# Keys and queries stored in residue order for dilated attention, stores issued one step later, and the last tiles finished by feature quarters

## The chip, the core and the metric

The kernel runs on one core of a Trainium2 chip. The metric is device time in microseconds, the median of three runs. Engines are named as in the profile: PE is TensorE's matmul, PEld its weight load, DVE is VectorE, ACT is ScalarE, POOL is GpSimd, SP is the sync engine, whose queue issues nearly all DMAs of this kernel in order. L1077 is line 1077 of the kernel before the change. Beside the times there is one profiled execution, with its trace.

## What is computed

One layer of a hybrid decoder, in fp32, for a prompt of 2048 tokens and for eight single decode steps. The input projection gives attention queries, keys and values (6 heads of 64), the mLSTM's branch (4 heads of 160) and gates:

```python
z = rmsnorm(x, norm1_g) @ w_in
qa, ka, va, xb, ob, gates = jnp.split(z, SPLITS, axis=-1)
branches = [dilated_prompt(qa, ka, va, rel_bias, w, d) for (w, d) in ((128, 1), (512, 4), (2048, 16))]
out_a = rmsnorm(combine_branches(branches).reshape(B, S, D_A), attn_out_g)
```

A branch with dilation d regroups the positions by their residue modulo d. Within a residue, every block of 128 queries attends to its own block and the one before it, with a causal band, a relative-position bias and a softmax; the three branches are merged by their softmax denominators. The other half of the features goes through a causal convolution and an mLSTM in 16 chunks of 128 tokens. Both halves go through w_out, then a feed-forward part with squared ReLU (1024 to 4096 to 1024) and a last rmsnorm. Outputs are y for both inputs and the new caches (keys, values, convolution and mLSTM state).

## The kernel before

Matrix products in fp32 are made from fp32r parts: a value is split into a high and a low part (`split`), and `mm3` issues three matmuls, high by high, high by low and low by high. A tile framework allocates buffers by name with a number of slots, adds the semaphores and orders the instructions; instructions under `pinned` keep the program's order.

The work goes through these stages, in microseconds of the profiled execution:

- 0 to 103, `norm_and_v`: norm, transposes, values. Each of 16 tiles stores its values at once, to the scratch tensor `v_d` (65 columns a head, the last one 1.0) and to the output (L867, L868).
- 103 to 242, `project_qk` (L913 to L977): three 128-row weight tiles for keys, then three for queries, each over the six column blocks of `BLK` (344 or 340 tokens). A block is 24 matmuls into a PSUM slot (four slots). ACT copies it out, `split` or the like makes `hi` and `lo` (two buffers each), and two DMAs store them to `k_d` or `q_d`, which hold 384 rows by 2048 tokens in natural order, one tensor for the high and one for the low part. Keys are also transposed (`to_rows`, a block later) and stored as an output. The bias tables (`setup_bias`) and the gates (`setup_gates`) are made in between.
- 242 to 402, `xbob(0)`: the mLSTM's input and output-gate projections for the first 1024 tokens, with convolution and gates on DVE and ACT, and stores after each block (L1002, L1027, L1035, L1036); the decode steps' attention runs beside it.
- 402 to 578, `xbob(1)`: the same for the rest, with three steps of `attention` between its blocks.
- 578 to about 1025, `mlstm`: 16 chunks, with the rest of `attention` in between (0.72 attention steps a step of the mLSTM). A chunk loads its slices and two broadcast rows (`Mb`, `wr`), and stores its result `G2c` to `oB_d` (L491).
- 1009 to 1252: output projection, norm and transposes for the feed-forward part.
- 1252 to 2586: the feed-forward part by a seven-product scheme for 2 x 2 blocks (`PROD_A`, `PROD_B`, `PROD_C`), in two halves of tokens; pinned steps with a hand-written look-ahead (`ahead`), and background jobs (`bg`) popped between steps.
- 2586 to 2607: the last five tiles are finished.

`attention` goes over 6 heads, for each over branches 2, 1, 0 (dilations 16, 4, 1), for each over 4 groups of 4 tiles, two tiles a step. `load_head` loads a head's `Q2` (64 rows of the high part over 64 rows of the low part), `KH` (the high part twice) and `KL` (the low part twice), two buffers each, when the head before begins its last branch. `front` makes the scores of a tile with two matmuls of 256 columns (L1077) that pick the positions of a residue by a stride:

```python
mv, out, c0 = K[:, a - P * d:a + (P - 1) * d + 1:d], s_[:, e], 0
pe.matmul(out, Q[:, a:a + (P - 1) * d + 1:d], mv, start=i == 0, stop=i == 1)
```

Where a tile has only its own block (the first block of a residue, all tiles at dilation 16), two neighbouring residues are computed and one is used, to keep 256 columns. DVE adds the bias and takes the minimum (L1079), ACT takes the exponential (L1081), `turn` transposes on PE (L1090) and copies (L1092), `weigh` multiplies with `V` (L1105), and every fourth tile ACT copies to `R4` (L1107, three buffers) and a DMA stores it (L1108). A group's `V` is loaded at its start (L1128, four buffers). A step's weigh comes three steps after its scores.

At the end, the accumulator `acc` of the feed-forward part holds features by rows; a tile of 128 tokens is transposed back in two halves of 512 features and added to x (`half`, L1595 and L1597), then `final` takes the square sum (L1603), the root, the scaling by root and gain (L1609, or L1606 with L1607 on GpSimd for every second of the last five), and stores (L1610). The last product, number 7, completes features 0 to 511 of tiles 8 to 12; features 512 to 1023 of these tiles are complete after product 4 and are added in the background.

## Time and profile before

| | |
|---|---|
| median of three runs | 2617.8 us (2612.7, 2617.8, 2622.02) |
| profiled execution | 2609.03 us |
| its span, first to last instruction | 2607.3 us |
| mean granted TensorE clock | 0.982 |
| DMA traffic | 491.13 MB, mean 188 GB/s |

The profile lists for each engine its busy time; for a line and operation, the number of instructions, their busy time, their mean duration, and the idle time of the engine just before them with what ended it. A window gives busy time by engine in a stretch, the granted clock, the mean busy share of the 16 DMA engines and the rate. A busy matmul is counted from the start to a modelled end, so neighbouring ones overlap. The queue's own waits say what held SP back before it could issue.

### The profile page before, as it was taken

The page shows a single profiled execution, that of the slowest core. Times are in us where ns is not written, and L with a number is a line of the kernel's source. Part 1 is how long each engine was busy: PE and PEld are TensorE (multiplying, and loading weights), DVE is VectorE, ACT ScalarE, POOL GpSimd, SP SyncE. Part 2 cuts the span into 40 slices and gives each one's busy share as a digit, 9 for nine tenths or more (in the row PEclk, how much of TensorE's full clock was granted, in tenths as well). Part 3 has the DMA queues.
Part 4 walks back from the last instruction along what each step waited for, and adds up shares of the span by engine and source line. Part 5 has one row for each costly group of instructions (what it writes and reads, how often), then busy time and mean ns, then how long its engine had stood idle before and what let it go on. Part 6 is the DMA issues. An engine that isn't in the chain of part 4 may idle for free. (4 is left out here: it accounts for less than half of the span.)

```text
span 2607.3 us, 41900 instructions
## 1 busy us (share of the span) xinstructions
PE 2502.6 (96%) x15646; PEld 2259.5 (87%) x15646; DVE 1762.1 (68%) x3146; ACT 1190.7 (46%) x2324; POOL 861.9 (33%) x435
## 2 busy tenths in 40 slices
PE   8999999999999998999999999999999999999996
PEld 7989999997888886788788878877799999999995
DVE  6333755663876567664476997779868777776875
ACT  6331223433445544455566435553345643456333
POOL 1000000002432323211345775447743333543331
PEclk9999999998999998999999999999999999999998
DMA  7674656736768744865676868768576543765332
GB/s 200 156 194 150 178 137 175 186 98 150 186 174 190 170 127 140 269 221 169 211 263 213 289 226 273 234 207 296 205 265 240 186 133 96 241 216 170 109 118 74
DMA packets 471727, 491.13 MB, mean 188 GB/s; under 512 B 117399, under 2 KB 388147, under 8 KB 467812
## 3 DMA queue, kind: packets, MB, share of 16 engines
q1 hardware_dynamic: 469700, 484.84, 61.5%
q0 software_dynamic: 1536, 3.10, 0.5%
q8 instruction: 123, 2.02, 0.3%
q14 instruction: 80, 0.66, 0.1%
q10 hardware_dynamic: 288, 0.53, 0.1%
HBM read 379.97 MB, written 124.56 MB: 194 GB/s over the span
## 5 line engine op out<-in xcount | busy, mean ns | idle before, releaser
L74 DVE TENSOR_TENSOR al<-ax,ah 128x1024 fp32r<-128x1024 f32 x222 | 413.2, 1864 | 151.5 <-ACT ah L74 150.9
L74 POOL TENSOR_TENSOR ax<-ax,ay 128x1024 f32<-128x1024 f32 x117 | 313.6, 2682 | 309.1 <-DMA ay<-in_w_ff_dram 267.6
L1583 PE MATMUL pf<-bl,ah 128*128 128x258 f32 (+1 forms) x1344 | 361.1, 323 | 11.5 <-DVE bl L74 11.5
L1549 PE MATMUL pf<-bh,ah 128*128 128x258 f32 (+1 forms) x1344 | 360.4, 323 | 11.6 <-DVE R L74 11.1
L1549 PE MATMUL pf<-bh,al 128*128 128x258 f32 (+1 forms) x1344 | 357.9, 321 | 2.0 <-DVE al L74 2.0
L1583 PE MATMUL pf<-bh,al 128*128 128x258 f32 (+1 forms) x1344 | 358.9, 321 | 0.0
L1549 PE MATMUL pf<-bl,ah 128*128 128x258 f32 (+1 forms) x1344 | 358.3, 321 | 0.0
L1583 PE MATMUL pf<-bh,ah 128*128 128x258 f32 (+1 forms) x1344 | 351.9, 323 | 4.6 <-ACT bh L74 2.9
L74 ACT ACTIVATE ah<-ax 128x1024 fp32r<-128x1024 f32 x222 | 234.0, 1055 | 236.7 <-PE pf L1583 123.7
L74 POOL TENSOR_TENSOR bx<-R,R 128x1024 f32<-128x1024 f32 (+1 forms) x80 | 243.8, 3054 | 259.2 <-DVE bl L74 259.2
L74 DVE TENSOR_TENSOR bl<-bx,bh 128x1024 fp32r<-128x1024 f32 (+1 forms) x131 | 273.6, 2092 | 35.7 <-ACT bh L74 35.1
L1583 PEld LDWEIGHTS pf<-bl,ah 128*128 128x128 f32 x1344 | 225.4, 191 | 33.4 <-DVE bl L74 14.1
L1549 PEld LDWEIGHTS pf<-bh,ah 128*128 128x128 f32 x1344 | 224.6, 190 | 32.4 <-issue 10.2
L163 PE MATMUL pmm<-x,wh 128*128 128x344 f32 (+1 forms) x768 | 250.6, 326 | 0.0
L165 PE MATMUL pmm<-x,wl 128*128 128x344 f32 (+1 forms) x768 | 247.8, 323 | 0.0
L1583 PEld LDWEIGHTS pf<-bh,ah 128*128 128x128 f32 x1344 | 224.1, 190 | 27.1 <-ACT bh L74 3.8
L164 PE MATMUL pmm<-x,wh 128*128 128x344 f32 (+1 forms) x768 | 247.4, 322 | 0.0
L1549 PEld LDWEIGHTS pf<-bh,al 128*128 128x128 f32 x1344 | 224.2, 190 | 22.4 <-DVE al L74 2.7
L1549 PEld LDWEIGHTS pf<-bl,ah 128*128 128x128 f32 x1344 | 225.2, 191 | 19.4
L1583 PEld LDWEIGHTS pf<-bh,al 128*128 128x128 f32 x1344 | 224.7, 190 | 19.2
L74 ACT ACTIVATE R<-R 128x512 f32<-128x512 f32 (+1 forms) x256 | 161.1, 630 | 131.1 <-DVE R L74 127.1
L74 DVE TENSOR_TENSOR R<-R,pf 128x512 f32<-128x512 f32 (+1 forms) x256 | 164.9, 681 | 51.5 <-PE pf L1549 38.0
(472 smaller groups left out, 4845.0 us busy)
## 6 DMA issues: line engine op xcount, KB each, us to landing
ax<-in_w_ff_dram SPq DMA_DIRECT2D x184, 512.0 KB
ay<-in_w_ff_dram SPq DMA_DIRECT2D x120, 512.0 KB
sum_d<-ax SPq DMA_DIRECT2D x40, 512.0 KB
ax<-sum_d SPq DMA_DIRECT2D x40, 512.0 KB
xt<-in_x_prompt_dram SPq DMA_DIRECT2D x31, 512.0 KB
bx<-h_d SPq DMA_DIRECT2D x26, 516.0 KB
bx<-h_d SPq DMA_DIRECT2D x26, 512.0 KB
by<-h_d SPq DMA_DIRECT2D x22, 516.0 KB
```

The costliest lines, as they stand in the source:

```text
L74: return tc.keep_in_program_order(f(*a, **k))
L163: pe.matmul(out, lh, rh, start=first, stop=False)
L164: pe.matmul(out, lh, rl, start=False, stop=False)
L165: pe.matmul(out, ll, rh, start=False, stop=last)
L1549: pe.matmul(pf[:, n, :w], x_, y_[:, n * w:n * w + w], start=fst, stop=lst)
L1583: pe.matmul(pf[:, n, :w], x_[:, i, dsl], y_[:, n * w:n * w + w], start=a, stop=b)
```

## The change

- **Residue order.** `k_d` gets two versions, natural and regrouped by 16 residues within every 512 tokens; `q_d` gets three: natural, regrouped by 4 within 512, and regrouped by 16 over all 2048. `project_qk` makes them with copies on ACT (high part) and DVE (low part) and stores them all. The column blocks become 512 wide (the last one 256 and 264, with the eight decode tokens).
- **Attention reads.** The weights of a score matmul are always `Q[:, a:a + P]`, contiguous. Keys of dilation 4 and 16 are read in runs of 32 elements. At dilation 4 the keys then come in another order within a block, so `V` is loaded by four DMAs in that order, and the bias is reordered by one ACT copy a head.
- **Loads.** Q is loaded once a branch, K twice a head, each at group 1 of the branch before. `V` is loaded a group ahead (six buffers).
- **Stores later.** A class `Stores` holds store DMAs and issues them one step later in the projections (`vst`, `qst`, `xst`), in attention (`rst`) and in the mLSTM (`obs`). `R4` gets four buffers, `G2c` three, `wr` two; the transposed keys `kt` get one.
- **The end.** For tiles 8 to 12 the square sum is taken by parts (`sq3`). Features 512 to 1023 are added after product 4, features 0 to 255 after the first half of product 7's steps, with GpSimd multiplying both by the gain; features 256 to 511 are left for the end. One root serves all five tiles; the scaling is one instruction a tile, three on DVE and two on ACT. Up to three background jobs a step instead of two.

```diff
-    q_d = [dram.tile([DA, S], F32, name=f"q{x}_d") for x in "hl"]
-    k_d = [dram.tile([DA, S], F32, name=f"k{x}_d") for x in "hl"]
+    q_d, k_d = ([[dram.tile([DA, S], F32, name=f"{y}{x}{v}_d") for x in "hl"] for v in range(n)]
+                for y, n in (("q", 3), ("k", 2)))
+    class Stores:
+        def put(self, dst, src):
+            self.held.append((dst, src))
+        def go(self):
+            for dst, src in self.held:
+                nc.sync.dma_start(dst, src)
+            self.held = []
...
-        G2 = wk.tile([P, 5, P], F32, name="G2c")
+        G2 = wk.tile([P, 5, P], F32, name="G2c", bufs=3)
-            wr = wk.tile([P, H, P], F32, name="wr", bufs=1)
+            wr = wk.tile([P, H, P], F32, name="wr")
-        nc.sync.dma_start(cm_(oB_d)[:, :, ts], G2)
+        obs.put(cm_(oB_d)[:, :, ts], G2)
...
+                    for c0, n in ((0, 512),) if g < 3 else ((0, 256), (256, 264)):
+                        ps = proj(psm, "mm", wh, wl, b0 + c0, n)
+                        if not c0:
+                            qst.go()
+                        if later:
+                            to_rows(*later.pop())
...
+                    d = 16 if which == "k" else 4
+                    hd_ = ev.tile([P, 512], F32R, name="qhd")
+                    ld_ = ev.tile([P, 512], F32R, name="qld")
+                    act.activation(on(hd_, d), by(hi, d).bitcast(F32), AF.Copy)
+                    vec.tensor_copy(on(ld_, d), by(lo, d).bitcast(F32))
+                    for v, two in enumerate(((hi, lo), (hd_, ld_))):
+                        for dd, tt in zip(dst[v], two):
+                            qst.put(dd[j * P:(j + 1) * P, b0:b0 + 512], tt.bitcast(F32))
+                    if which == "q":
+                        if g == 3:
+                            q16 = [ev16.tile([P, 16, P], F32R, name=f"q16{x}") for x in "hl"]
+                        act.activation(q16[0][:, :, 32 * g:32 * g + 32], by(hi, 16).bitcast(F32), AF.Copy)
+                        vec.tensor_copy(q16[1][:, :, 32 * g:32 * g + 32], by(lo, 16).bitcast(F32))
...
-                    if w == 256:
-                        mv, out, c0 = K[:, a - P * d:a + (P - 1) * d + 1:d], s_[:, e], 0
+                    q = Q[:, a:a + P]
+                    if b == 0:
+                        mv = K[:, max(a - P, 0):max(a - P, 0) + 256]
+                    elif b == 1:
+                        g, t = a // 512, a % 512 // P
+                        if w == 256:
+                            mv = g44(K)[:, g - 1:g + 1, :, t]
+                            out = out.rearrange("p (k r z) -> p k r z", k=2, r=4)
...
+                        mv = g4(K)[:, :, a // P - e:a // P - e + 2].rearrange("p g r z -> p r g z")
-                    pe.matmul(out, Q[:, a:a + (P - 1) * d + 1:d], mv, start=i == 0, stop=i == 1)
+                    pe.matmul(out, q, mv, start=i == 0, stop=i == 1)
...
+                    if g == 1:
+                        if b:
+                            qq = load_q(h, b - 1)
+                        if b == 2:
+                            kk[0] = load_k(h, 0)
+                        elif b == 0 and h + 1 < HA:
+                            nb, kk[1], qq = load_bias_of(h + 1), load_k(h + 1, 1), load_q(h + 1, 2)
+                    V, vnext = vnext, load_group(*groups.pop(0)) if groups else None
+                    R4 = wk.tile([P, 4, HD + 2], F32, name="R4", bufs=4)
...
+            if ready and p == 7 and d["ds"][0] == 2 and not d["end"]:
+                bg.extend(ready)
+                ready.clear()
-            for _ in range(2 if sb and c and ph == 2 else 1):
+            for _ in range(3 if sb and c and ph == 2 else 1):
...
+                    def most(t, add=add):
+                        add(t, (0, 1))
+                        for xv, gv in ((xts[t][:, :256], fg[:, :256]), (xts[t][:, 512:], fg[:, 512:])):
+                            gp.tensor_tensor(xv, xv, gv, op=OP.mult)
...
                     for t in early:
-                        half(xts[t], acc, base, t, 0)
-                        final(xts[t], t, t % 2 == 1)
+                        add(t, (2, 3))
+                    v = small.tile([P, NE], F32, name="rs_v5")
+                    vec.tensor_tensor(v, sq3[:, 0], sq3[:, 1], op=OP.add)
+                    vec.tensor_tensor(v, v, sq3[:, 2], op=OP.add)
+                    vec.tensor_scalar(v, v, 1.0 / D, EPS, op0=OP.mult, op1=OP.add)
+                    r = rsqrt(v, P, NE)
+                    for t in early:
+                        xv = xts[t][:, 256:512]
+                        vec.tensor_tensor(xv, xv, fg[:, 256:512], op=OP.mult)
+                    for t in early:
+                        x_, k = xts[t], t - 8
+                        if k % 2:
+                            act.activation(x_, x_, AF.Copy, scale=r[:, k:k + 1])
+                        else:
+                            vec.tensor_scalar(x_, x_, r[:, k:k + 1], None, op0=OP.mult)
+                        nc.sync.dma_start(O["y_prompt"][0, t * P:t * P + P], x_)
```

More of the change, by code (lines that the diff above doesn't have):

```diff
@@ new lines, in project_qk @@
+                for g in (range(4) if which == "k" else (3, 0, 1, 2)):
+                    b0 = 512 * g
+                    hi = ev.tile([P, 512], F32R, name="qhi")
+                    lo = ev.tile([P, 512], F32R, name="qlo")
+                    qb = None
+                    if which == "k" or g == 3:
+                        qb = ev.tile([P, 520], F32, name="qb", bufs=3)
+                    for c0, n in ((0, 512),) if g < 3 else ((0, 256), (256, 264)):
[4 more added lines that the diff above has]
+                            to_rows(*later.pop())
+                        m = min(n, 512 - c0)
+                        cs = slice(c0, c0 + m)
+                        if which == "k":
+                            act.activation(qb[:, c0:c0 + n], ps[:, :n], AF.Copy)
+                            split(hi[:, cs], lo[:, cs], qb[:, cs])
+                        else:
+                            act.activation(hi[:, cs], ps[:, :m], AF.Copy, scale=-0.125)
+                            vec.scalar_tensor_tensor(lo[:, cs], ps[:, :m], -0.125, hi[:, cs].bitcast(F32),
+                                                     op0=OP.mult, op1=OP.subtract)
+                            if n > m:
+                                act.activation(qb[:, 512:], ps[:, m:n], AF.Copy, scale=-0.125)
+                    d = 16 if which == "k" else 4
[7 more added lines that the diff above has]
+                    if which == "q":
+                        if g == 3:
+                            q16 = [ev16.tile([P, 16, P], F32R, name=f"q16{x}") for x in "hl"]
+                        act.activation(q16[0][:, :, 32 * g:32 * g + 32], by(hi, 16).bitcast(F32), AF.Copy)
+                        vec.tensor_copy(q16[1][:, :, 32 * g:32 * g + 32], by(lo, 16).bitcast(F32))
+                        if g == 2:
+                            for dd, tt in zip(dst[2], q16):
+                                qst.put(dd[j * P:(j + 1) * P], tt.rearrange("p r z -> p (r z)").bitcast(F32))
+                    if qb is not None:
+                        later.append((which, j, g, qb))
@@ L1001, in xbob @@
                 vec.tensor_copy(halo[:, j], xb[:, m:m + 3])
-                nc.sync.dma_start(xbT_d[j * P:(j + 1) * P, b0:b0 + m], xb[:, 3:3 + m])
+                xst.put(xbT_d[j * P:(j + 1) * P, b0:b0 + m], xb[:, 3:3 + m])
                 c = ev.tile([P, 344], F32, name="c")
@@ L1060, in rows, with load_v @@
             return bass.AP(tensor=t.tensor, offset=t.offset + row * rs + off, ap=[[st[0], P], [st[1], 4], [1, w]])
+        def load_v(V, b, g, h):
+            if b == 1:
+                rs = HD + 1
+                for r in range(4):
+                    nc.sync.dma_start(V[32 * r:32 * r + 32],
+                                      bass.AP(tensor=v_d.tensor, offset=v_d.offset + (h * S + 512 * g + 4 * r) * rs,
+                                              ap=[[16 * rs, 32], [rs, 4], [1, rs]]))
+            else:
+                nc.sync.dma_start(V, rows(v_d, b, g, HD + 1, h * S * (HD + 1), HD + 1))
         def front(hd, b, tiles):
-            nb, Q, KH, KL = hd
-            d = BRANCHES[b][1]
+            nb, (KH, KL), Q = hd
             o, bw = NBW[b]
+            g4 = lambda t: t.rearrange("p (g r z) -> p g r z", r=16, z=32)
+            g44 = lambda t: t.rearrange("p (g k r z) -> p g k r z", k=4, r=4, z=32)
             ex = wk.tile([P, 2, 256], F32, name="ex", bufs=3)
@@ L1107, in weigh, with load_group @@
                 act.activation(R4[:, :, :HD + 1], po, AF.Copy)
-                nc.sync.dma_start(dst, R4)
-        hd = load_head(0)
+                rst.put(dst, R4)
+        nb, kk, qq = load_bias_of(0), {1: load_k(0, 1)}, load_q(0, 2)
         pend, turned, acc_o, DEPTH = [], [], [None], 2
+        rst = Stores()
+        def load_group(h, b, g):
+            V = wk.tile([P, 4, HD + 1], F32, name="V", bufs=6)
+            load_v(V, b, g, h)
+            return V
+        groups = [(h, b, g) for h in range(HA) for b in (2, 1, 0) for g in range(4)]
+        vnext = load_group(*groups.pop(0))
         def flush():
@@ L1149, in attention @@
             flush()
+        rst.go()
         yield
@@ L1193, in mlstm @@
                 next(cur)
+                if not i:
+                    obs.go()
                 if i and prev is not None:
@@ L1642, in phase_c @@
         copies = cache_copies()
-        bg = []
+        NE = 5
+        sq3 = pc.tile([P, 3, NE], F32, name="sq3")
+        bg, ready = [], []
         acc = None
```

166 lines of the change are left out of this document (81 added, 85 removed).

## The prediction

> **What bounds the kernel now.** I read the page first, then busy time by stage, then the score matmuls of attention by themselves, then the sync queue's own waits, and last the end of the span. The page gives the span
>
> ```profile
> span 2607.3 us, 41900 instructions
> ```
>
> and the busy time, share and instructions of each engine:
>
> ```profile
> PE 2502.6 (96%) x15646; PEld 2259.5 (87%) x15646; DVE 1762.1 (68%) x3146; ACT 1190.7 (46%) x2324; POOL 861.9 (33%) x435
> ```
>
> TensorE is busy for all but 105 us. That says only that it rarely sits idle: a matmul that reads its operands slowly is busy too. So the question for each stage is whether TensorE leaves time over there, and whether its work gets shorter. Stages, with the sync and DMA side in the last two columns (share of the 16 DMA engines, GB/s):
>
> ```profile
> core 0: us, PE busy (x) PEld busy (x) DVE busy (x) ACT busy (x) POOL busy (x), PEclk, DMA share, GB/s
> 103.00:242.00 139.00, 133.45 (x856) 130.36 (x856) 37.23 (x108) 39.12 (x103) 4.68 (x9) 0.99 0.62 172
> 242.00:402.00 160.00, 159.25 (x1031) 158.44 (x1031) 102.59 (x247) 40.63 (x76) 0.00 (x0) 0.98 0.60 170
> 402.00:580.00 178.00, 176.48 (x1146) 172.49 (x1145) 107.62 (x381) 66.58 (x150) 3.06 (x6) 1.00 0.57 144
> 580.00:700.00 120.00, 111.39 (x708) 92.13 (x707) 67.24 (x241) 51.81 (x154) 34.30 (x33) 0.90 0.66 159
> 700.00:850.00 150.00, 144.74 (x1010) 130.65 (x1010) 105.65 (x359) 75.93 (x238) 55.20 (x49) 0.99 0.76 188
> 850.00:1000.00 150.00, 141.55 (x1004) 127.57 (x1002) 89.03 (x313) 72.38 (x218) 39.16 (x36) 0.98 0.57 140
> ...
> 2400.00:2586.00 186.00, 178.98 (x1460) 177.37 (x1459) 136.18 (x138) 65.63 (x78) 56.94 (x18) 0.98 0.30 97
> 2586.00:2607.00 21.00, 3.32 (x23) 2.19 (x21) 12.30 (x29) 8.74 (x22) 5.25 (x2) 0.70 0.31 125
> ```
>
> 103 to 242 projects keys and queries, 242 to 402 is the first half of the other projections, 402 to 1000 holds attention (beside the second half of the projections, then beside the mLSTM), 2586 to 2607 is the tail after the last FFN matmul. Added over its four rows, attention keeps TensorE busy 574 of 598 us and VectorE 370: TensorE is the bound, and a microsecond taken from its work there is nearly a microsecond of the span.
>
> **Part 1: scores read in residue order.** Attention's score matmuls (L1077) are the same in number and shape in all three branches; only the strides differ. Their busy time, summed over six stretches, one a head, with dilation 16:
>
> ```profile
> sum 200.40, PE 71.06 PEld 49.68; mean PE 11.84 PEld 8.28
> ```
>
> with dilation 4:
>
> ```profile
> sum 193.80, PE 73.94 PEld 51.56; mean PE 12.32 PEld 8.59
> ```
>
> and with dilation 1:
>
> ```profile
> sum 199.80, PE 49.46 PEld 31.17; mean PE 8.24 PEld 5.19
> ```
>
> One head at dilation 4 (min/median/max ns, first and last start):
>
> ```profile
> L1077 PE MATMUL ps_s<-KL,Q x16: 407/416/422, 424.8 to 457.8; 128*128 128x256 f32 x16
> L1077 PEld LDWEIGHTS ps_s<-KL,Q x15: 332/332/335, 426.4 to 457.6; 128*128 128x128 f32 x15
> ```
>
> and at dilation 1:
>
> ```profile
> L1077 PE MATMUL ps_s<-KL,Q x17: 278/282/418, 457.8 to 490.8; 128*128 128x256 f32 x17
> L1077 PEld LDWEIGHTS ps_s<-KL,Q x16: 187/192/193, 458.4 to 490.7; 128*128 128x128 f32 x16
> ```
>
> A strided matmul takes 416 instead of 282 ns, its weight load 332 instead of 192. After the change the queries of every branch are contiguous, and the keys of dilations 4 and 16 come in runs of 32. If both branches then cost what dilation 1 costs, the saving is 71.06 + 73.94 - 2 x 49.46 = 46.1 us. No row shows runs of 32, so the bounds are the two rows above: 282 ns (all 46.1 saved) and 416 ns (nothing saved). I take the near end: 31 of 32 steps are the unit steps of the 282 ns row, and the extra 134 ns over 256 columns, 0.5 ns a strided step, would add 4 ns for eight jumps.
>
> The Trainium skill, page "SBUF — State Buffer", section "Door 1: The DMA port swizzle", states 16-byte lines and that four fp32 can be strided for free. Read so, stride 4 would have nothing to give and the saving would be 71.06 - 49.46 = 21.6 us; the 416 ns row at stride 4 contradicts it, and the measurement decides.
>
> What comes late next is VectorE's bias-and-minimum (L1079), which frees the score buffers. Idle time before L1077 from 402 to 1000, matmul and weight load added up:
>
> ```profile
>   DVE R L1079: 21.3, 27
> ```
>
> Nearly all of it lies in the dilation-1 stretches, where scores are already quick; counted twice by that row, it is some 10 us for the engine. Dilation 4 has the same tiles of 256 keys and will show the like, dilation 16 half the keys and little: I give back 6 us (0 to 10). Net of part 1: -40.
>
> **Part 2: the projection of keys and queries.** For each of six weight tiles, six blocks of up to 344 columns become three of 512, one of 256 and one of 264: 24 matmuls of 144 fewer, but the same columns. A 344-column matmul takes 160 / 1031 = 155 ns (row 242 to 402), 0.45 ns a column; a 512-column one in the FFN
>
> ```profile
> 1252.00:1410.00 158.00, 157.93 (x689) 127.35 (x688) 108.55 (x110) 100.33 (x156) 72.11 (x28) 1.00 0.72 238
> ```
>
> 229 ns, 0.45 ns too. Time goes by columns, so I count 1 us saved (0 to 22, if it went by number). VectorE and ScalarE get the reordering copies. Nearest rows:
>
> ```profile
> L160 DVE TENSOR_TENSOR qlo<-qb,qhi 128x344 fp32r<-128x344 f32 (+1 forms) x18 | 9.4, 522 | 44.5 <-ACT qhi L159 27.1 <-DMA kl_d<-qlo 17.3
> L956 ACT ACTIVATE qb<-pmm 128x344 f32<-128x344 f32 (+1 forms) x18 | 8.2, 456 | 41.6 <-PE pmm L165 41.6
> ```
>
> Per 512 columns that is about 0.75 us; 36 copies on each engine (12 key blocks, 24 for queries) make 27 us, on VectorE 37 + 27 of 139, on ScalarE 39 + 27. Even at twice the price TensorE covers them: nothing on the path.
>
> The stores are another matter. Keys go out twice and queries three times, each as high and low part of 384 x 2048 fp32 (3.15 MB): 31.5 MB instead of 12.6. The stage moves 172 GB/s at a share of 0.62, so its full rate is 277 GB/s, and 18.9 MB more are 68 us of all engines against 0.38 x 139 = 53 us free. The stage is then DMA-bound by up to 15 us, unless stores drain into the next one, whose share is 0.60. The row of L160 above already shows 17.3 us of VectorE waiting for a store to land without TensorE stopping (four PSUM slots lie between). I take +7 (0 to 23, the upper end with 8 us for weights of the next stage that queue behind the last stores).
>
> **Part 3: loads of attention.** Before, a head loads KH and, with the same counts, KL, and Q from its high and its low part:
>
> ```profile
> KH<-kh_d SPq DMA_DIRECT2D x12, 512.0 KB
> ...
> Q<-qh_d SPq DMA_DIRECT2D x6, 512.0 KB
> ```
>
> That is 6 x 0.524 = 3.15 MB a head. After: three Q and two pairs of K, 14 transfers, 7.34 MB; 25.2 MB more over six heads. Two wider windows:
>
> ```profile
> 402.00:1000.00 598.00, 574.16 (x3862) 522.85 (x3860) 369.54 (x1292) 266.70 (x758) 131.72 (x123) 0.97 0.64 157
> 712.00:867.00 155.00, 149.93 (x1031) 135.08 (x1031) 105.34 (x365) 75.67 (x236) 52.77 (x48) 0.99 0.76 182
> ```
>
> 157 GB/s at 0.64 is 245 GB/s at full share: 103 us more, on 0.36 x 598 = 215 us free. On average the share goes to about 0.87. From 712 to 867 it is 0.76 already, and 1.7 heads' worth of loads there would fill it. I charge +8 (0 to 25) for loads that come late in that stretch.
>
> **Part 4: stores one step later, V a group ahead, second buffers.** The sync queue issues in order, and a store that waits for its data holds the loads behind it. Its own waits from 580 to 1000:
>
> ```profile
> SPq L1108 <- ACT R L1107: 62.1, 18, 7.4
> SPq L491 <- POOL G2c L490: 50.7, 13, 6.9
> SPq L1128 <- PE po L1105: 38.6, 14, 6.1
> SPq L405 <- POOL wz L434: 21.0, 7, 7.0
> ```
>
> Those are the attention and mLSTM stores, the V load (four buffers, now six) and the decay row (one buffer, now two): all four are what the change moves. The queue gets some 48 more K and Q transfers and 72 more V transfers (dilation 4 in four pieces), which it has time for once 172 us of waiting shrink. TensorE sat idle 8.6 + 5.3 + 8.5 = 22 us in those stages (120 - 111.39, 150 - 144.74, 150 - 141.55), not all of it from late loads; I take -4 (0 to -12). From 242 to 580 TensorE idles 2.3 us, so the delayed projection stores win nothing there. Nothing computes longer because a store goes later: the store's tile is held one step longer, and G2c and R4 get a buffer more for it.
>
> **Part 5: the end in feature quarters.** Tail of before:
>
> ```profile
> L1603 ACT ACTIVATE jkc<-R 128x1024 bf16<-128x1024 f32 x5 | 5.3, 1050 | 19.9 <-DVE R L1597 19.9
> L1607 POOL TENSOR_TENSOR R<-R,g 128x1024 f32<-128x1024 f32 x2 | 5.3, 2626 | 31.9 <-ACT R L1606 31.9
> L1609 DVE SCALAR_TENSOR_TENSOR R<-R,rs_o,g 128x1024 f32<-128x1024 f32 x3 | 3.9, 1285 | 0.1
> L1597 DVE TENSOR_TENSOR R<-R,ptp 128x512 f32<-128x512 f32 x5 | 3.3, 684 | 0.7 <-PE ptp L1595 0.6
> L139 DVE TENSOR_SCALAR rs_v<-ss 128x1 f32<-128x1 f32 x5 | 0.8, 150 | 0.6 <-ACT jkc L1603 0.6
> ```
>
> and its last instruction by time:
>
> ```profile
> 2600.05 2.38 POOL L1607 TENSOR_TENSOR R<-R,g 128x1024 f32<-128x1024 f32 x1 [1.66 <-ACT R L1606]
> ```
>
> The last multiply ends at 2602.4, 4.9 us before the span does (the store). New tail after the last matmul at about 2586.3: the last put into the accumulator and transposes 1.2; five adds of 256 features at about 0.4, 2.0; the last square of a quarter row 0.65; one root for all tiles, nine small steps at 0.15 to 0.2, 1.8; five gain multiplies of 256 at 0.35, 1.8; scaling, three tiles on VectorE at no more than 1.29, 3.9, with two on ScalarE beside them; the store 4.9. Together 16.3 instead of 21.0. GpSimd multiplies three quarters of each tile, 0.75 x 2.63 = 2.0 us, 10 for five, hidden behind the last two steps (48 matmuls each at 178.98 / 1460 = 0.12 us, 5.9 us) and the adds; without that cover 4 us of it would show. Ten transposes move ahead of the last matmul (1.4 us at the 3.32 / 23 of the row 2586 to 2607), but three background jobs a step instead of two end the earlier tiles sooner, where TensorE now idles 7 us (186 - 178.98). I take -5 (+1 to -10).
>
> **Sum.** -46 + 6 - 1 + 7 + 8 - 4 - 5 = -35 us. The profiled execution took 2609.0 us, 1.7 of it outside its span, so it would become 2574. The runs shown have a median of 2617.8, 8.8 above it; the prediction for the median is 2617.8 - 35 = 2583.
>
> **The rivals.** *The transfers stay hidden and waits vanish.* For it: shares on average below 0.9, and a sync queue that no longer blocks. Against: 712 to 867. -46 - 1 - 8 (tail) - 7 (idle) = -62: 2556.
>
> *Slower: loads queue behind bursts.* Per head there are two bursts of 3.15 MB (keys of the next order with queries), 12.9 us each at 245 GB/s. Whatever is issued behind one, V or an mLSTM chunk's tiles, lands that much later; the lead is one group, a quarter of a dilation's 193.80 / 6 = 32 us, 8 us. If the consumers really have no more lead than that, each of 12 bursts stops TensorE for 5 us: +60, and with +15 in the projection the sum is -46 + 6 - 1 + 15 + 60 - 4 - 5 = +25: 2643. It decides where a burst is longer than the lead. For it, GpSimd waits for mLSTM loads today:
>
> ```profile
> POOL Mb L399 <- DMA Mb<-MtT_d: 64.7, 11, 32.9
> ```
>
> Against: V is used some three half groups after its scores, so its lead is nearer 20 us, and today's burst at a head's start is as long.
> The Trainium skill, "SBUF — State Buffer", same section, gives a 64-partition transfer only half of the ports, 196 GB/s at 1 MiB; each K and Q transfer has 64 partitions, and a burst would be an estimated 16 us. No view here isolates such a transfer.
>
> *The runs of 32 cost what strides cost.* Then part 1 is 0 and the rest +5: 2623.
>
> **How the numbers follow.** This measurement tells about 0.3% from no change, 7.9 us: below 2610 is faster, above 2626 slower. Forecast (-22 to -50 us, 2568 to 2596): 0.60. All hidden: 0.13. A smaller gain (2596 to 2610), where DMA takes half: 0.08. Bursts decide: 0.11, from +8 up in nearly all of it. Runs as slow as strides: 0.08, mostly within 0.3%. Faster 0.81, same 0.08, slower 0.11. The range, 2556 to 2612, leaves out the last two cases and a little of the second.
>
> **What would show it.** Right: score matmuls of all branches near 282 ns and about 150 us in three sums of 49; the stretch from 402 to 1000 some 40 us shorter with VectorE busier in share; DMA share near 0.9 there and above 0.85 from 103 to 242; the span's end some 16 us after the last FFN matmul. Wrong: score matmuls still above 350 ns (runs), or TensorE idle growing by over 30 us between 402 and 1000 with GpSimd or VectorE waiting for loads (bursts), or the projection of keys and queries over 155 us.

## The result, and the profile after

The change makes the kernel slower: 2641.3 us, median of 4 runs (2636.0 to 2644.5), against 2617.7; ratio 1.0108, 95% interval 1.0086 to 1.0129. The prediction said 2583 and faster. The profiled execution took 2644.5 us. Page of the kernel after, span and busy time:

```profile
span 2642.8 us, 41794 instructions
PE 2495.9 (94%) x15496; PEld 2216.9 (84%) x15496; DVE 1741.1 (66%) x3173; ACT 1236.8 (47%) x2345; POOL 875.4 (33%) x443
```

TensorE is 6.7 us less busy than before, in a span that is 35.5 us longer: the work shrank and the idle time grew. The stretch from the first to the last score matmul (402 to 995 before, 416 to 1044 now), first before, and then after, there with the two stages ahead of it and the end:

```profile
402.00:995.00 593.00, 569.16 (x3827) 517.96 (x3825) 366.62 (x1284) 265.80 (x756) 131.72 (x123) 0.97 0.64 158
```

```profile
103.00:256.00 153.00, 149.07 (x798) 125.69 (x797) 57.30 (x139) 74.28 (x108) 4.69 (x9) 0.97 0.80 259
256.00:416.00 160.00, 153.96 (x963) 151.95 (x962) 101.42 (x242) 43.40 (x77) 0.00 (x0) 0.95 0.70 192
416.00:1044.00 628.00, 555.24 (x3799) 489.30 (x3798) 352.67 (x1279) 270.17 (x759) 129.13 (x121) 0.90 0.78 187
2626.00:2643.00 17.00, 2.36 (x14) 1.15 (x12) 8.05 (x23) 6.17 (x18) 1.41 (x2) 0.69 0.39 154
```

The first score comes 14 us later (402.5, then 416.7), the score stretch takes 35 us more, and what follows the last score takes 13 us less (1612.1, then 1598.7), of which 4 are the end (no run shows where the other 9 come from). In the score stretch TensorE's idle time goes from 23.8 to 72.8 us, its granted clock from 0.97 to 0.90, and the share of the DMA engines from 0.64 to 0.78. Yet the score matmuls themselves did what they should. Their busy time over the whole stretch (TensorE, then weight load), before and after:

```profile
402.00:995.00 593.00, 194.05 (x576) 132.29 (x576) 0.97 0.64 158
```

```profile
416.00:1044.00 628.00, 143.84 (x576) 94.42 (x576) 0.90 0.78 187
```

That is 50 us less, even at a lower clock, and the median score matmul with the low part of the keys takes the 282 ns of dilation 1 (min/median/max over all branches):

```profile
L1146 PE MATMUL ps_s<-KL,Q x288: 277/282/582, 416.9 to 1043.9; 128*128 128x256 f32 x144
```

So the forecast gain is there, and something took it and 35 us more. One gap shows how. The sync queue of the kernel after, with the start and length of each issue (rows between left out), and TensorE:

```profile
500.73 0.45 SPq L1097 DMA_DIRECT2D Q<-qh_d  x1
506.87 0.37 SPq L146 DMA_DIRECT2D R_d<-R  x1
507.29 0.50 SPq L1098 DMA_DIRECT2D Q<-ql_d  x1
...
510.07 0.45 SPq L1098 DMA_DIRECT2D KL<-kl_d  x1
510.58 0.68 SPq L1120 DMA_DIRECT2D V<-v_d  x1
```

```profile
516.00 0.33 PE L1159 MATMUL pt<-ident,ex 128*128 128x128 f32 x1
523.65 1.94 PE L1175 MATMUL po<-V,pT 128*128 128x65 f32 x8 [7.33 <-DMA V<-v_d]
```

Inside the burst of queries and keys the queue stands 5.7 us until a store can go (from 501.18 to 506.87), then issues the rest, and V behind it (issued at 510.58) lands 13 us later, at 523.5. TensorE stands 7.33 us, and starts again at half clock with the DMA engines full:

```profile
510.00:516.00 6.00, 5.93 (x48) 5.39 (x46) 3.66 (x19) 3.79 (x12) 0.00 (x0) 1.00 0.97 220
516.00:523.60 7.60, 0.33 (x2) 0.13 (x1) 0.43 (x1) 0.22 (x1) 0.00 (x0) 0.73 1.06 220
523.60:530.00 6.40, 4.60 (x16) 4.01 (x17) 2.36 (x2) 2.36 (x3) 0.00 (x0) 0.50 1.06 271
```

Only few gaps are as plain as this one. The waits of the score stretch, kernel after (total, times, longest):

```profile
POOL hb L493 <- DVE hrd L490: 96.6, 12, 22.1
POOL Mb L413 <- DMA Mb<-MtT_d: 59.8, 9, 14.2
PE ps_s L1146 <- DVE R L1148: 32.0, 34, 3.8
PE po L1175 <- DMA V<-v_d: 10.8, 3, 7.3
```

TensorE's own longest wait is for VectorE's bias-and-minimum (L1148): 32.0 us here, 8.8 before. VectorE is busy 352.67 us of 628, so it waits in its turn, and the view doesn't say what stands first in that row. GpSimd's wait for the mLSTM's loads (`Mb`) hasn't grown: it is 59.8 us here, and the prediction shows 64.7 before.

### The profile page after: what moved, and what is told of

It is laid out like the page before. It is cut to its first block, busy times and chain, and to the rows that moved or that the text cites. A ratio compares the mean times of both kernels' runs of the same rounds, so it can differ in the third digit from the quotient of the medians.

```text
span 2642.8 us, 41794 instructions
## 1 busy us (share of the span) xinstructions
PE 2495.9 (94%) x15496; PEld 2216.9 (84%) x15496; DVE 1741.1 (66%) x3173; ACT 1236.8 (47%) x2345; POOL 875.4 (33%) x443
## 5 line engine op out<-in xcount | busy, mean ns | idle before, releaser
L74 DVE TENSOR_TENSOR al<-ax,ah 128x1024 fp32r<-128x1024 f32 x222 | 396.3, 1788 | 169.4 <-ACT ah L74 168.6
L175 PE MATMUL pmm<-x,wh 128*128 128x344 f32 (+4 forms) x720 | 245.6, 341 | 2.4 <-ACT wh L171 2.4
L177 PE MATMUL pmm<-x,wl 128*128 128x344 f32 (+4 forms) x720 | 243.4, 338 | 0.6 <-DVE wl L172 0.6
L176 PE MATMUL pmm<-x,wh 128*128 128x344 f32 (+4 forms) x720 | 242.4, 337 | 0.0
L1150 ACT ACTIVATE ex<-sm,R 128x256 f32<-128x256 f32 (+1 forms) x288 | 128.1, 458 | 170.9 <-DVE R L1148 146.6
```

The lines of the kernel that those rows point to most:

```text
L74: return tc.keep_in_program_order(f(*a, **k))
L175: pe.matmul(out, lh, rh, start=first, stop=False)
L176: pe.matmul(out, lh, rl, start=False, stop=False)
L177: pe.matmul(out, ll, rh, start=False, stop=last)
L1150: act.activation(ex[:, e, :w], sm[:, :w], AF.Exp, bias=mn, scale=-1.0)
```

## The experiments

Three theories. **Transfers**: the 25.2 MB of extra key and query loads make other transfers late, TensorE stands, and its clock falls in the gaps. **Chains**: shorter scores only uncover the mLSTM's root and VectorE's queue; the loads don't matter. **Held buffers**: a store one step later holds its buffer and reorders the queue. All runs; the stretch is from the first to the last score matmul, with TensorE's busy time, clock and the DMA share in it. A ratio compares with runs of before made beside that kernel; their median was 2617.7 beside after and 2607.6 to 2613.5 beside the others. So where the text takes the difference of two medians of different rounds, it can be off by some us:

| kernel | median us | ratio to before, 95% | stretch | busy | clock | DMA |
|---|---|---|---|---|---|---|
| before | | | 402 to 995 | 569 | 0.97 | 0.64 |
| after | 2641.3 | 1.0108 (1.0086, 1.0129) | 416 to 1044 | 555 | 0.90 | 0.78 |
| loads once | 2584.5 | 0.9893 (0.9870, 0.9917) | 415 to 975 | 523 | 0.95 | 0.68 |
| reads only | 2570.8 | 0.9842 (0.9817, 0.9867) | 401 to 956 | 524 | 0.96 | 0.67 |
| end only | 2611.5 | 0.9995 (0.9977, 1.0012) | 407 to 1004 | 572 | 0.97 | 0.63 |
| stores at once | 2676.9 | 1.0252 (1.0222, 1.0283) | 416 to 1078 | 571 | 0.88 | 0.75 |
| one order | 2599.1 | 0.9955 (0.9933, 0.9977) | 414 to 998 | 554 | 0.96 | 0.66 |
| the same, stores at once | 2611.0 | 0.9997 (0.9979, 1.0015) | 412 to 1000 | 555 | 0.95 | 0.64 |
| spread | 2673.1 | 1.0248 (1.0209, 1.0287) | 415 to 1071 | 574 | 0.90 | 0.77 |
| other queue | 2696.9 | 1.0326 (1.0289, 1.0363) | 421 to 1078 | 564 | 0.88 | 0.75 |
| three queries | 2627.0 | 1.0048 (1.0028, 1.0068) | 415 to 1016 | 563 | 0.95 | 0.73 |
| dummy transfers | 2612.7 | 1.0021 (1.0000, 1.0041) | 414 to 1013 | 543 | 0.93 | 0.74 |
| dummies, other queue | 2637.8 | 1.0107 (1.0075, 1.0139) | 465 to 1026 | 526 | 0.95 | 0.68 |
| reorder on chip | 2596.9 | 0.9947 (0.9926, 0.9968) | 402 to 986 | 558 | 0.96 | 0.63 |
| the same, blocks of before | 2593.0 | 0.9938 (0.9915, 0.9962) | 403 to 986 | 555 | 0.97 | 0.64 |
| both in order | 2584.4 | 0.9884 (0.9867, 0.9901) | 407 to 970 | 526 | 0.96 | 0.67 |
| the same, on GpSimd | 2586.1 | 0.9894 (0.9879, 0.9910) | 407 to 982 | 532 | 0.96 | 0.65 |
| both in order, small buffers | 2573.5 | 0.9875 (0.9851, 0.9899) | 402 to 964 | 526 | 0.96 | 0.68 |

**Loads once.**

```diff
-                cur = nb, kk[min(b, 1)], qq
+                cur = nb, kk[1], qq
...
-                        if b:
-                            qq = load_q(h, b - 1)
-                        if b == 2:
-                            kk[0] = load_k(h, 0)
-                        elif b == 0 and h + 1 < HA:
+                        if b == 0 and h + 1 < HA:
```

> After the change, but each head loads one K and one Q version (3.15 MB a head, as before) instead of three of each (7.34 MB); the scores of dilations 4 and 1 are of other positions, everything else is issued as after. Transfers theory (small loads and stores land late behind the extra key and query loads, and TensorE's clock falls in the gaps): 30 to 40 us shorter than after, near 2605. Chain theory (the shorter scores only uncover the root of the mLSTM and VectorE's queue; the loads don't matter): within 8 us of after's 2641. Held-buffer theory (stores one step later hold R and the load buffers): within 8 us of after.

2584.5: 57 us shorter than after. Without the extra loads the score stretch drops from 628 to 560 us, and both parts of the loss shrink: TensorE idles 36.8 us there instead of 72.8, and is busy 523.2 instead of 555.2, at a clock of 0.95 instead of 0.90:

```profile
415.00:975.00 560.00, 523.16 (x3791) 470.09 (x3790) 359.13 (x1286) 266.31 (x760) 131.47 (x123) 0.95 0.68 166
```

Chains and held buffers would have kept the time. It is also more than the 30 to 40 us expected. The wait for L1148 falls from 32.0 to 16.3 us.

**Reads only** (before, with one edit).

```diff
...
+                    a0 = (a, a // 512 * 512 + a % 512 * P, a * P)[b]
+                    k0 = max(a0 - P, 0)
+                    mv, out, c0 = K[:, k0:k0 + 256], s_[:, e], e * P if b and w < 256 else 0
+                    pe.matmul(out, Q[:, a0:a0 + P], mv, start=i == 0, stop=i == 1)
```

> Before the change, with the one edit that every score matmul reads queries and keys side by side from the natural order (so the scores of dilations 4 and 16 are of other positions); no extra load, no extra store, no deferral. Transfers theory: the whole gain of the reads comes through, about 40 us shorter than before, near 2578. Chain theory: less than 15 us shorter, with TensorE idle over 20 us more than before between the first score and the last, and its clock lower there. Held-buffer theory: as the transfers theory, about 40 us shorter.

42.7 us shorter than before: the gain of the reads (part 1) is what the prediction said, -40, and the chains don't take it back. TensorE idles 30.6 us in the stretch against 23.8.

**End only** (before, with the change's end).

```diff
-                        half(x_, acc, base, t, 1)
+                        add(t, (4, 5, 6, 7))
...
+                    ready.extend(lambda t=t: most(t) for t in early)
```

> Before the change, with only the end in feature quarters. All theories: 4 to 8 us shorter than before (the end after the last FFN matmul 21.0 to about 17), near 2612; the attention stage as before.

From the last FFN matmul to the span's end it is 16.7 us (2592.8 to 2609.5), as forecast, but the time as a whole can't be told from before.

**Stores at once** (after, without the deferral).

```diff
         def put(self, dst, src):
-            self.held.append((dst, src))
+            nc.sync.dma_start(dst, src)
```

> After the change, with every store issued at once instead of one step later; key and query order, V a group ahead and the second buffers stay. Held-buffer theory: 10 us or more shorter than after, near 2630. Transfers theory and chain theory: within 8 us of after's 2641, or longer by the waits that the deferral was to avoid.

35.6 us longer than after. The deferral doesn't cost, so held buffers are out; it saves, and three times as much as the prediction's bound.

**One order of keys and queries**, the candidate without extra bytes: dilation 1 reads the residue-ordered keys in runs of 8, the queries are strided in the weight load.

```diff
+                    q = Q[:, a0:a0 + (P - 1) * d + 1:d]
                     if b == 0:
-                        mv = K[:, max(a - P, 0):max(a - P, 0) + 256]
+                        m = max(a // P - 1, 0)
+                        mv = bass.AP(tensor=K.tensor, offset=K.offset + m // 4 * 512 + m % 4 * 8,
+                                     ap=[list(K.ap[0]), [488 if m % 4 == 3 else 8, 2], [32, 16], [1, 8]])
...
```

> After the change, but with one order of each: keys in residue order only, queries in natural order only (the strides of 4 and 16 stay in the weight loads of the score matmuls); dilation 1 reads its keys in runs of 8 out of the residue order, its bias is put in that order and its exp writes back in the natural one. Loads of a head 3.15 MB and stores of queries and keys as before the change; deferral, V a group ahead, second buffers and the end stay. Transfers theory, with the stride of the moving keys as what cost before: 2565 to 2580, the score matmuls 119 to 122 ns apart in all branches, and the attention starts near 403 instead of 417. If it was the strided weight load that cost, dilations 4 and 16 stay 219 to 233 ns apart and the time is 2600 to 2615. If runs of 8 cost as much as a stride, dilation 1 goes to about 220 ns apart and the time is 2580 to 2600.

2599: 12 us faster than before, but not by the reads. At dilation 4 with keys in runs of 32 and strided queries (min/median/max ns):

```profile
L1140 PEld LDWEIGHTS ps_s<-KH,Q x14: 308/309/333, 431.8 to 461.7; 128*128 128x128 f32 x14
L1140 PE MATMUL ps_s<-KL,Q x15: 386/397/401, 430.7 to 462.0; 128*128 128x256 f32 x15
```

The strided weight load alone keeps the old cost (median distance of the matmuls' ends 222 ns at dilation 16 and 235 at 4; 119 at dilation 1, so runs of 8 are free).

**The same with stores at once** (the edit of above).

> The kernel with one order of keys and queries, with every store issued at once instead of one step later: what the deferral is worth when the loads are as light as before. The run of after with stores at once was 35 us longer than after; with light loads I expect 10 to 35 us longer than the same kernel with deferral if waiting stores hold up the loads behind them in SyncE's queue, and under 5 us if the deferral only mattered because of the extra loads.

12 us longer: with light loads the deferral is worth 12, with the change's loads 36.

**Spread**: one 512 KB piece a step.

```diff
...
+                        if todo and (g or i):
+                            nc.sync.dma_start(*todo.pop(0))
```

> After the change, with the same key and query loads issued one 512 KB piece a step (from the first step of a branch on) instead of six pieces at once. If small transfers suffer because they queue behind a burst: 20 us or more shorter than after's 2641, and the waits for V and for the mLSTM's loads gone. If the sum of bytes is what costs (the queues are near full whatever the order): within 8 us of after.

32 us longer than after, where neither theory put it. It isn't a clean test of the burst, since the pieces now come last in a queue that stands at stores for longer, while their consumer is near. Kernel with spread loads, waits of the sync queue from 592 to 1000:

```profile
SPq L146 <- ACT R L1179: 106.1, 19, 18.6
```

The same line of after has 58.0 us, longest 8.7. Here the early burst did better than the late pieces; what spreading with the same lead would do, no run shows.

**Other queue.**

```diff
-                nc.sync.dma_start(dst[:HD], lo[hs])
+                nc.scalar.dma_start(dst[:HD], lo[hs])
...
```

> After the change, with the key and query loads issued from ScalarE's queue instead of SyncE's, all else as after. If what costs is the order within SyncE's one queue (V, mLSTM loads and stores behind 3.15 MB): 20 us or more shorter than after. If the sum of bytes costs: within 8 us of after, or longer by what the issuing and its waits cost ScalarE.

56 us longer than after. ScalarE now stands at the buffers' waits in its own order, ahead of its exps: TensorE waits 26.1 us for exps there, five times, up to 8.4 us (0.6 us in after). So this too mixes two effects; the dummies below leave the buffers' waits out.

**Three queries**: a dose between.

```diff
-                for y, n in (("q", 3), ("k", 2)))
+                for y, n in (("q", 3), ("k", 1)))
...
```

> After the change, with the queries in their three orders as there, but keys in natural order alone, loaded once a head and read with the strides of 4 and 16 as before the change: 5.24 MB of loads a head, between 3.15 and 7.34. If only the strided weight load (the queries) cost time, dilations 4 and 16 come 119 to 122 ns apart; if the strided keys cost too, over 200. Transfers theory with a cost in proportion to the bytes: half way between the run with loads once (2584.5) and after (2641), near 2612. With a cost that begins only near the limit of the queues: 2585 to 2595.

2627.0, above both forecasts and 28 us over the kernel with one order (24 by the ratios), which has one operand strided as well, for 2.1 MB more a head (and the stores of them); after's 4.2 MB cost 57. By the medians half the loads cost half, about 2.2 us a MB. The score stretch of the profiled execution doesn't bear that out (kernel with one order, then this one):

```profile
414.00:998.00 584.00, 554.37 (x3800) 505.70 (x3799) 360.53 (x1286) 286.93 (x765) 131.20 (x123) 0.96 0.66 160
415.00:1016.00 601.00, 562.57 (x3796) 497.83 (x3795) 355.56 (x1286) 267.05 (x755) 130.85 (x123) 0.95 0.73 176
```

It is 17 us longer, and so it is against reorder on chip, below, which has the same strides and takes 584 too. That is a quarter of the 68 (628 against 560) that the full loads cost there; the profiled execution is also the longest of this kernel's ten runs, and much of its excess lies behind the last score. So more bytes cost more, but two doses don't show whether in proportion, or with a cost that rises steeply toward a full queue. The distance of score matmuls is 220 ns at dilation 16 and 233 at 4: strided keys keep it over 200 with contiguous queries.

**Dummy transfers**: loads once, plus copies nobody waits for.

```diff
+        def dummy(h, k, srcs):
+            for x in srcs:
+                nc.sync.dma_start(scr[h, k], x[HD * h:HD * h + HD])
+                k += 1
...
```

> The kernel with loads once a head, plus copies of the same query and key rows from DRAM to DRAM, as many, as large and at the same places as the extra loads of after, that nobody waits for (scores of dilations 4 and 1 are of other positions). If the extra bytes cost by holding up the other transfers: 2620 to 2650, like after. If they cost because the key and query tiles themselves come late, or by another order of the instructions: 2583 to 2595, like the kernel with loads once (2584.5).

28 us longer than loads once (33 by the ratios), half of the 57 or a little more:

```profile
414.00:1013.00 599.00, 542.51 (x3794) 479.77 (x3793) 352.05 (x1280) 270.49 (x760) 128.52 (x121) 0.93 0.74 189
```

The stretch is 39 us longer than with loads once, at a lower clock: bytes that no instruction needs hold up those that are needed. The wait for L1148, 16.3 us with loads once, is 34.8 here. The rest of the 57 this run doesn't explain.

**Dummies from ScalarE's queue.**

```diff
-                nc.sync.dma_start(scr[h, k], x[HD * h:HD * h + HD])
+                nc.scalar.dma_start(scr[h, k], x[HD * h:HD * h + HD])
```

> The kernel with dummy transfers (2612.7), with the dummies issued from ScalarE's queue instead of SyncE's; they wait for no buffer. If what the extra bytes cost comes from the order within SyncE's queue (others behind them): near the kernel with loads once, 2585 to 2592. If it comes from sharing the engines that move the data: 2605 to 2620, as before.

2637.8, 53 over loads once. With no buffer to wait for they ran early, from about 130 to 435, and the loss moved with them. Kernel with dummies on the other queue:

```profile
250.00:300.00 50.00, 47.73 (x277) 43.81 (x275) 18.85 (x39) 18.71 (x26) 0.00 (x0) 1.00 1.02 358
300.00:350.00 50.00, 28.56 (x149) 27.71 (x150) 33.42 (x79) 6.93 (x14) 0.00 (x0) 0.76 0.83 251
465.00:1026.00 561.00, 525.79 (x3800) 471.86 (x3799) 360.38 (x1287) 267.08 (x760) 131.61 (x123) 0.95 0.68 166
```

From 250 to 300 the DMA engines are full at 358 GB/s, and from 300 to 350 TensorE is busy 28.56 us of 50; the first score comes at 465 instead of 415. The score stretch, free of dummies, takes 561 us like that of loads once. So the bytes cost without the sync queue's order. Whether they cost at the DMA engines or at the DRAM behind them no run separates, and what they cost depends on the stage that they fall into: here it is nearly all of the 57. The Trainium skill, page "DMA: Bandwidth & Descriptors", section "Issuing engines are not separate DMA queues", says that DMAs of several issuing engines end up on the same 16 engines; the trace agrees, with the 16 engines' share at 1.02 while ScalarE's queue adds to the sync queue's work, and moving transfers to ScalarE's queue gained nothing: the two runs took 25 and 56 us longer than from the sync queue.

**Reorder on chip**: natural order for both, ScalarE puts the queries in order a group ahead; keys strided.

```diff
+        def reorder(Q, b, g, i):
+            if i == 0:
+                qg[0] = wk.tile([P, 4, P], F32R, name="Qg")
+            src = (Q[:, 512 * g:512 * g + 512] if b == 1 else Q).rearrange("p (z r) -> p r z", z=P)
+            r = i if b == 1 else 4 * g + i
+            act.activation(qg[0][:, i:i + 2], src[:, r:r + 2], AF.Copy)
+            return qg[0]
...
```

> One order of queries and of keys, both natural, 3.15 MB of loads a head; the keys are read with their strides, and ScalarE puts the queries of dilations 4 and 16 in order in SBUF, half a group of 128x256 a step (96 copies of some 0.57 us, 55 us of ScalarE in 580), one group ahead. Deferral, V a group ahead, second buffers, projection in blocks of 512 and the end stay as after. If the strided weight load alone cost time and the extra transfers alone cost the gain: 42 us shorter than the kernel with one order (2599), near 2557 to 2570. If ScalarE becomes late (exp behind the copies): 2575 to 2600.

2596.9, not 2557 to 2570. At dilation 4, contiguous queries and strided keys:

```profile
L1107 PEld LDWEIGHTS ps_s<-KH,Qg x14: 186/188/209, 426.0 to 455.8; 128*128 128x128 f32 x14
L1107 PE MATMUL ps_s<-KL,Qg x15: 397/414/431, 424.7 to 456.2; 128*128 128x256 f32 x15
```

The weight load is quick, and the matmul is as slow as ever. Either stride alone costs all of it, so the view that only the weight load counts was wrong.

**The same with the projection of before** (blocks of 344, stores at once).

> The kernel with the reorder on chip, with the key and query projection as before the change (blocks of 344, stores at once). If the larger buffers of the projection in blocks of 512 keep out the loads for the sample attention (first cache load at 261 us in the kernel with one order, 183 before): the loads start near 183 again, the first score comes near 402 instead of 414, and the time is 8 to 13 us shorter than the kernel with reorder on chip. If not: within 4 us.

2593, within 4 us. The loads of the sample attention do start at 186 us instead of 255, but the projection ends 9 us later (259.0 against 250.1), so the two cancel.

**Both in order**: residue-ordered keys, written so by the split, and the reorder on chip.

```diff
+                    if which == "k":
+                        split(on(hi, 16), on(lo, 16), by(qb[:, :512], 16))
...
```

> One order of keys (residue order, written so by the split itself, without second tiles in the projection) and one of queries (natural), 3.15 MB of loads a head; ScalarE puts the queries of dilations 4 and 16 in order in SBUF a group ahead, dilation 1 reads the keys in runs of 8. So both operands of every score matmul lie side by side, which neither the kernel with one order (queries strided) nor the kernel with reorder on chip (keys strided) had. If both have to lie so: score matmuls 119 to 122 ns apart in all branches, and 35 to 45 us shorter than those two (2599 and 2597): 2552 to 2565. If the chains behind the scores take the gain: 2575 to 2600.

The distance is 119 or 120 ns in all branches, and the time 2584.4, not 2552 to 2565: 28 us faster than before, but only 13 to 15 less than its two halves (16 to 18 by the ratios). The stretch is 21 us shorter than theirs (563 against 584); TensorE idles 36.9 us in it against 25.6 with keys strided. That fits chains behind the scores that take part of the gain; no run isolates it.

**The same with the copies on GpSimd.**

```diff
-            act.activation(qg[0][:, i:i + 2], src[:, r:r + 2], AF.Copy)
+            gp.tensor_copy(qg[0][:, i:i + 2], src[:, r:r + 2])
```

> The kernel with both in order, with the copies that put the queries in order on GpSimd instead of ScalarE. If ScalarE's extra 55 us delay the exps: some 5 to 10 us shorter than with ScalarE. If a GpSimd copy is slow or holds up VectorE: 5 to 30 us longer.

2586.1, not to be told from ScalarE's: ScalarE's extra copies don't explain what is missing.

**Both in order, small buffers.**

```diff
-                        qb = ev.tile([P, 520], F32, name="qb", bufs=3)
+                        qb = ev.tile([P, 520], F32, name="qb", bufs=2)
...
-                    lo = ev.tile([P, 512], F32R, name="qlo")
+                    lo = ev.tile([P, 512], F32R, name="qlo", bufs=1)
```

> The kernel with both in order, with the buffers of the projection cut by 4.1 KB a partition (two instead of three of the raw block, one instead of two of the low part). If the size of these buffers is what keeps the sample attention's first loads out until the projection ends (and costs TensorE some 6 us idle at 325 us and the half clock behind it): the first cache load starts well before 255 us, the idle there is under 1.5 us, and the first score comes 5 to 10 us earlier than 406.9, if the projection itself does not wait for its fewer buffers; the time is 2574 to 2582. If not: 2580 to 2590, or more if the projection waits.

2573.5, 1.25% under before and the fastest median of the kernels that compute the right result. It can't be told from both in order, though: the intervals of the two ratios overlap (0.9875 and 0.9884). The first load of the sample attention's cache and the stretch that waits for it, in before (that load alone), in after, and in this kernel:

```profile
L520 SPq DMA_DIRECT2D kx<-in_cache_win_k_dram x8: 333/427/471, 183.0 to 260.3; - x8
```

```profile
L534 SPq DMA_DIRECT2D kx<-in_cache_win_k_dram x8: 421/440/462, 267.7 to 298.7; - x8
```

```profile
300.00:360.00 60.00, 54.41 (x319) 52.82 (x319) 33.54 (x84) 13.41 (x24) 0.00 (x0) 0.86 0.64 174
```

```profile
L534 SPq DMA_DIRECT2D kx<-in_cache_win_k_dram x8: 429/496/965, 185.0 to 270.7; - x8
```

```profile
300.00:360.00 60.00, 59.64 (x405) 59.26 (x403) 35.89 (x91) 14.53 (x27) 0.00 (x0) 1.00 0.50 142
```

With 4.1 KB less the loads start at 185 us instead of 261 in both in order (268 in after), TensorE no longer stands there (60 - 59.64 = 0.4 us idle, 5.6 in after), the granted clock in this stretch is 1.00 (0.86 in after), and the first score comes 4.7 us before that of both in order, although the projection, with fewer buffers, ends 5 us later.

## Why the prediction was wrong, point by point

- **Part 1** (-46, then 6 given back) was right: 50 us less busy time in the scores, and 42.7 us of the whole when done alone, against 40. The reason given for it, strides, holds too.
- **Part 3** (+8, 0 to 25) is the step that failed. I set 103 us of transfers against 215 us of free DMA time and charged only the stretch that would fill. Measured: 57 us by the medians, at a mean share of 0.78, where 0.87 was forecast. So the average never filled, and the step from free DMA time to a small cost is what was wrong. A mean share hides stretches at 0.97 to 1.06, such as the one in which V landed late. Idle time is not all of it either: against loads once, the score stretch has 36 us more idle time and 32 us more busy time, at a clock of 0.90 instead of 0.95.
- **The rival "loads queue behind bursts"** gave 2643, and 2641 was measured; I gave it 0.11 because V seemed to have 20 us of lead. That the number fits is luck. The plain case exists (13 us, 7.33 us of TensorE), but TensorE waits for V only 10.8 us in three places, not 12 times 5; the projection, which the rival charged with 15, ends no later; and GpSimd's wait for the mLSTM's loads didn't grow.
- **Part 2** (-1 and +7) lay in its range with the wrong cause; the first score came 14 us later. The projection's last matmul ends at 255.6 instead of 256.3 (not at 242: the stage table cuts before's projection short), with the DMA share at 0.80: the stores hid, as the lower bound said. The loss came after it: from 256 to 416 TensorE idles 6.0 us at a clock of 0.95, where before's row from 242 to 402 has 0.8 us and 0.98, which makes about 10 of the 14. The sample attention's loads, which start 85 us later, are the likely reason: larger and more projection tiles keep them out of SBUF (shown by taking buffers back in the last kernel, not in after itself). I had looked at times and queues, and not at what opens next in the same space.
- **Part 4** (-4, 0 to -12): the deferral alone is worth 12 with light loads and 36 with the change's. My bound was TensorE's idle time of before; but the deferral also takes away waits that the change itself adds. V a group ahead and the second buffers weren't tried by themselves.
- **Part 5** (-5): the end took 16.9 us (forecast 16.3, before 21.0); with only this edit the total moved by 2 us, within the interval.
- Of the sign that I named for being wrong, one half came: TensorE idles 49 us more in the attention. The other half came only in small part: GpSimd's wait for `Mb` is no longer than before, and VectorE's waits for transfers add up to 25 us in the score stretch, against 8 before.

What stays open: the part of the 57 us, up to half, that dummies from the sync queue don't cost. It may be the key and query tiles being late themselves, the sync queue standing at their buffers, or the new order of instructions, which differs between all these kernels; no run separates the three; and the dummies write to DRAM where the loads write to SBUF. How the cost grows with the bytes is open too. Nor does any run show why the fast reads bring 43 us alone and only 13 to 15 on top of the deferral.

## What to carry to other kernels

A transfer isn't free because the mean DMA share leaves room: price extra bytes beside a chain of small, awaited loads by a run with dummy copies, and take the answer as a part of the price (here 28 of 57 us for 25.2 MB). If the order of data in SBUF is what makes a matmul slow, put both operands in order once on chip, or change the order of the loop that writes them, before storing several versions in DRAM. When tiles grow, look at which pool opens next in the same space and what its first loads were waiting for.

## What the runs showed of the hardware

- Either operand's stride alone costs as much as both: the median distance between score matmuls is 222 to 235 ns with only queries strided, 220 to 233 with only keys, 218 to 233 with both (before), and 119 to 120 with neither; runs of 32 and of 8 fp32 cost nothing. I had put it down to one of the two. The Trainium skill, "TensorE: Matmul & The Clock Gate", section "Back-to-back issue gap", says that the distance is set by weight load and matmul together, pipelined; here the costs of the two strides don't add up.
- The granted clock falls to 0.50 in stretches of 3.4 us and multiples of it, mostly behind idle time of TensorE. Over the span it is 0.982 in the profiled execution before and 0.965 after, which is (1 - 0.982) x 2 x 2607.3 = 94 us at half clock, and 185. The same page, section "HAM oscillation — how this bites in real kernels", warns of idle gaps beyond about 3.4 us; the 7.33 us gap with 0.50 behind it agrees. But in before a gap of 1.99 us, the only idle time from 632 to 642, also has half clock behind it, and so have 10 us with 0.1 us of idle time; the measurement decides, and no run shows the rule behind it:

```profile
632.00:642.00 10.00, 8.01 (x47) 4.14 (x46) 1.52 (x7) 3.73 (x13) 2.91 (x5) 1.00 0.78 200
642.00:645.40 3.40, 3.40 (x19) 3.40 (x18) 1.50 (x7) 1.57 (x6) 1.03 (x2) 0.51 0.55 154
318.00:328.00 10.00, 9.89 (x69) 9.55 (x69) 8.00 (x24) 3.80 (x7) 0.00 (x0) 1.00 0.47 139
328.00:331.40 3.40, 3.40 (x14) 3.40 (x13) 0.16 (x1) 0.00 (x0) 0.00 (x0) 0.50 0.65 212
```
